# One layer of a hybrid encoder on one core: plain transposes in the input norm, a later hand-over of the state-space pieces, their output block in fixed order on another queue, and the first row tile's split in two parts

## The chip, the cores and the metric

One Trainium2 chip, one core. The metric is device time in microseconds of one execution; the kernel before took 1969.1 us, the median of three runs (1964.49 to 1969.29). The engines go by these names: PE or TensorE (matmul), DVE or VectorE, ACT or ScalarE, POOL or GpSimd, SP or SyncE (which issues most transfers). PSUM, where matmuls leave their results, has eight banks of 128 x 512 f32.

## The reference, cut to what matters

The input is 1024 rows of 1024 numbers. One layer is computed, in f32:

```
xn = rmsnorm(x) * g                       # over each row
p  = xn @ W_in                            # 1024 x 4896, cut into parts
y1 = S5(p[0:256]);  y2 = RG_LRU(p[256:768]);  y3 = GLA(p[768:1824])
merged = sum_b sigmoid(p_gate_b) * (y_b @ W_up_b)
h = x + merged @ W_mix_out
h = h + expert_choice_swiglu(rmsnorm(h))  # 16 experts, 128 rows each
out = rmsnorm(h)
```

S5, the state-space mixer, scans the sequence in both directions for 16 groups of 16 channels with 64 complex states each. Its output block is z = gelu(y), then z * sigmoid(z @ w_glu).

## The kernel before, in words

All of it is one function, written with a tile framework: the code issues instructions in a program order, and a planner puts them into each engine's queue when the program is built. It goes by priority (program order, unless a block says high priority) and by its own costs for when an instruction could start. Each engine then runs its queue strictly in that order, each instruction waiting for what it needs, and a transfer is issued from the queue of the engine that the code names. Inside a block marked `manual_schedule` each engine keeps the order of the code among the block's instructions; where instructions from outside the block come in between stays the planner's choice. Matmuls with f32 accuracy are made of three products of operands split into a high and a low part (`split`, line 52: ScalarE makes the high part, VectorE subtracts it).

**Prologue (lines 135 to 196, in manual order).** SyncE loads the rows x in four transfers of two 128-row tiles, then two 128-column blocks of W_in. For each row ScalarE sums squares (`sqs`, 143), VectorE adds epsilon and GpSimd raises to the power -0.5 (`chain`, 148; the power at line 81). Then VectorE makes a 128x128 tile `dg` for each row tile: the identity with the rows' factors on the diagonal (154). `xchunk(h, k)` (157) multiplies four 128x128 blocks of x with `dg` on TensorE (161), which transposes and scales at once, into one PSUM tile of 128x512 (`mx`, four buffers); ScalarE and VectorE split it into xnH and xnL (163). There are 16 chunks, eight for each half of the rows. Squares and chains for the second half stand between chunks of the first half, and the chain for the last four row tiles comes at once.

**Projections (line 380).** `proj` multiplies 128 columns of W_in with all rows: eight steps of k, three products, two halves, 48 matmuls into one of two PSUM tiles `pj`. `wsplit` (131) loads and splits the weights of the next one at high priority, and ScalarE evacuates the result (`evac`, 400, high priority), which SyncE stores to DRAM.

**State-space pieces (lines 486 to 654).** After the two projections for S5, a list of 13 tasks is driven: six projections for GLA, one larger one for its values (`col_va`), four for the LRU, two for the first gates. Behind each task `drive` (478) takes six pieces from the generator `s5_gen` (625). A batch of S5 has eleven: three that prepare coefficients on GpSimd and VectorE (`prep`, 505), then in `s5_batch` (530) transposes of W, small products that ScalarE copies out and SyncE stores as KD (567), loads of a Toeplitz tile TO from KD (571), state products, rotations, scans, rotations back, and the output products (609 and 615) with `Z` (620). Four batches, then the output block (631 to 652): gelu on Z in ScalarE, eight stores to ZD and one load back in another layout, both through SyncE, two f32 matmuls with w_glu for each half (643), tanh, a product, and the split into two `y` pairs. The first up-projection (`s5_out`, 676, matmuls at line 396) needs both.

**The end of the mixer (lines 973 to 1070).** Eight gates and up-projections of the LRU add to `merged` (128 x 8 x 1024, features in partitions). For the last feature block the addition is done first for the first 128 rows, then for the rest (1055 to 1058), and `msplit(t)` (1050) splits one 128-row tile of all eight feature blocks into MH and ML. The matmuls with W_mix_out start with tile 0 and feature block 0 (1087, matmuls at lines 68 to 70). The PSUM pools of the mixer are given back just before, and those of the next stage take their banks.

Behind it come router, selection of rows, and 16 experts with weights streamed from DRAM.

Of the kernel before, what the change touches and what calls it, by code (L numbers as in the profile page):

```python
# [8 lines left out]
F32 = mybir.dt.float32  # L9
# [3 lines left out]
AF = mybir.ActivationFunctionType  # L13
# [4 lines left out]
P = 128  # L18
S = 1024
D = 1024  # L20
KT = D // P
NT = S // P
# [15 lines left out]
def dram(t, off, ap):  # L38
    return bass.AP(tensor=t.tensor, offset=t.offset + off, ap=ap)
# [3 lines left out]
def hybrid_encoder(ctx: ExitStack, tc: tile.TileContext, A, out, dbg=None):  # L43
    nc = tc.nc
    v, g, s, te = nc.vector, nc.gpsimd, nc.scalar, nc.tensor
    dma = nc.sync.dma_start
    MUL, ADD, SUB = OP.mult, OP.add, OP.subtract

    def tap(name, ap):
# [3 lines left out]
    def act(o, i, f, bias=0.0, scale=1.0, **k):  # L53
        return s.activation(o, i, f, bias=bias, scale=scale, **k)  # L54

    def stt(o, a, c, b, op0, op1):
        return v.scalar_tensor_tensor(o, a, c, b, op0=op0, op1=op1)

    def split(h, lo, src, scale=None, eng=None):
        if scale is None:  # L60
            act(h, src, AF.Copy)
            (eng or v).tensor_tensor(lo, src, h.bitcast(F32), SUB)  # L62
        else:
            act(h, src, AF.Copy, scale=scale)
            stt(lo, src, scale, h.bitcast(F32), MUL, SUB)
# [13 lines left out]
    def rpow(o, x):  # L79

        g.tensor_tensor(o, x, mhalf.to_broadcast(list(x.shape)), OP.pow)
# [11 lines left out]
    def mx():  # L93
        return psum.tile([P, 512], F32, name="mx", bufs=4)
# [3 lines left out]
    idn = consts.tile([P, P], F32, name="idn")  # L98
# [7 lines left out]
    def ytile():  # L106
        return ypool.tile([P, S], F32R, name="y")
# [4 lines left out]
    xload = xlctx.enter_context(tc.tile_pool(name="xload", bufs=1, side="right", reuse_waits="tile"))  # L112
    x = A["x"][0]
    X = xload.tile([P, NT, D], F32, name="X")

    def xdma(t):
        dma(X[:, t:t + 2], x[t * P:(t + 2) * P].rearrange("(t p) d -> p t d", p=P))


    def wload(src, n):  # L120
        raw = xw.tile([P, KT, P], F32, name="wraw", bufs=2)
        dma(raw[:, :n], src.rearrange("(k p) c -> p k c", p=P))
        return raw, n

    def wconv(raw, n, eng=None):
        wh = xw.tile([P, KT, P], F32R, name="wh", bufs=2)
        wl = xw.tile([P, KT, P], F32R, name="wl", bufs=2)
        split(wh[:, :n], wl[:, :n], raw[:, :n], eng=eng)
        return wh, wl
# [8 lines left out]
    xnH = xw.tile([P, KT, S], F32R, name="xnH")  # L138
    xnL = xw.tile([P, KT, S], F32R, name="xnL")
    ss, rstd = (consts.tile([P, NT], F32, name=n) for n in ("ss", "rstd"))  # L140
    dg, first = [], []

    def sqs(t):
        for j in range(2):
            sq = xload.tile([P, D], F32, name="sq", bufs=2)
            act(sq, X[:, t + j], AF.Square, scale=1.0 / 32, accum_out=ss[:, t + j:t + j + 1])

    def chain(t, n):
        c = slice(t, t + n)
        v.tensor_scalar(ss[:, c], ss[:, c], EPS, None, op0=ADD)  # L150
        rpow(rstd[:, c], ss[:, c])
        for j in range(n):
            d_ = xload.tile([P, P], F32, name="dg", bufs=NT)
            v.tensor_scalar(d_, idn, rstd[:, t + j:t + j + 1], None, op0=MUL)
            dg.append(d_)

    def xchunk(h, k):
        hs = slice(h * 512, h * 512 + 512)
        ps = mx()
        for j in range(4):  # L160
            te.matmul(ps[:, j * P:(j + 1) * P], X[:, 4 * h + j, k * P:(k + 1) * P], dg[4 * h + j],
                      start=True, stop=True)
        split(xnH[:, k, hs], xnL[:, k, hs], ps, scale=gmix[:, k:k + 1])

    with tc.manual_schedule():
        dma(grow, A["mix_norm_g"].rearrange("l (k c) -> (l k) c", c=P))
        for t in range(0, NT, 2):
            xdma(t)
        raw0 = [wload(win[:, j * P:(j + 1) * P], KT) for j in range(2)]
        ps = mx()  # L170
        te.transpose(ps[:, 0:KT], grow, idn[:KT, :KT])
        v.tensor_copy(gmix, ps[:, 0:KT])
        for t in (0, 2):
            sqs(t)
            chain(t, 2)
        sqs(4)
        xchunk(0, 0)
        sqs(6)
        xchunk(0, 1)
        xchunk(0, 2)  # L180
        xchunk(0, 3)
        xchunk(0, 4)
        chain(4, 4)
        xchunk(0, 5)
        xchunk(0, 6)
        xchunk(0, 7)
        first.append(wconv(*raw0[0], eng=None))
        xchunk(1, 0)
        xchunk(1, 1)
        xchunk(1, 2)  # L190
        xchunk(1, 3)
        xchunk(1, 4)
        xchunk(1, 5)
        xchunk(1, 6)
        xchunk(1, 7)
        first.append(wconv(*raw0[1], eng=None))
    tap("xnH", xnH.bitcast(F32))
    tap("xnL", xnL.bitcast(F32))
# [31 lines left out]
    ps = mx()  # L230
# [7 lines left out]
    def tt(e, o, a, b, op=MUL):  # L238
        e.tensor_tensor(o, a, b, op)  # L239
# [35 lines left out]
    ps = mx()  # L275
# [55 lines left out]
    for n, src, sg in (("WR", PWR, 1), ("WI", PWI, 1), ("CR", PWR, 1), ("CI", PWI, 1), ("CN", PWI, -1)):  # L331
        t = sp.tile([P, 16, 8], F32, name="pq" + n)
# [29 lines left out]
    for n, sg in (("re", 1.0), ("im", -1.0)):  # L362
        ps = mx()
# [16 lines left out]
    def proj(c0):  # L380
        wh, wl = first.pop(0) if first else wsplit(win[:, c0:c0 + P], KT)
        ps = pj()
        for k in range(KT):
            for i, (w, xx) in enumerate(((wh, xnL), (wh, xnH), (wl, xnH))):
                for h in range(2):
                    te.matmul(ps[:, h], w[:, k], xx[:, k, h * 512:(h + 1) * 512],  # L386
                              start=(k == 0 and i == 0), stop=(k == KT - 1 and i == 2))
        return ps
# [11 lines left out]
    def evac(ps, dst, n=P):  # L400
        with tc.high_priority():
            ev = xw.tile([P, S], F32, name="ev", bufs=2)
            act(ev[:n], ps.rearrange("p a b -> p (a b)")[:n], AF.Copy)
            dma(dst, ev[:n])
# [3 lines left out]
    ZD = dpool.tile([256, 8, P], F32, name="ZD")  # L408
# [66 lines left out]
                "p (n s) -> p s n", s=8), AF.Copy)  # L475
            dma(UD[j * P:(j + 1) * P], ev.rearrange("p (s n) -> p s n", s=8))

    def drive(tasks, gen, n):
        for t in tasks:
            t()  # L480
            for _ in range(n):
                next(gen, None)
        for _ in gen:
            pass
# [3 lines left out]
    cols_rest = [lambda j=j: evac(proj(O_Q + j * P), GD[j * P:(j + 1) * P]) for j in (0, 1, 2, 3, 6, 7)]  # L488
# [6 lines left out]
    sw = s5ctx.enter_context(tc.tile_pool(name="s5w", bufs=1, side="right", reuse_waits="tile"))  # L495
# [3 lines left out]
    Z = sw.tile([P, 16, P], F32, name="Z")  # L499
# [125 lines left out]
    def s5_gen():  # L625
        for b in range(4):
            o = {}
            yield from prep(b, o)
            yield from s5_batch(b, o)
            yield  # L630
        act(Z, Z, AF.Gelu_apprx_tanh)
        for q in range(8):
            dma(dram(ZD, q * P, [[1024, 16], [16384, 16], [1, P]]), Z[q * 16:(q + 1) * 16])
        zT = sw.tile([P, 2, S], F32, name="Z")
        dma(zT, ZD.rearrange("(k p) t n -> p k (t n)", p=P))
        yield
        TT = sw.tile([P, 2, S], F32, name="U")
        for m in range(2):
            T = TT[:, m]
            for h in range(2):  # L640
                ps = mx()
                for k in range(2):
                    te.matmul(ps, wg[:, k, m * P:(m + 1) * P], zT[:, k, h * 512:(h + 1) * 512], start=not k, stop=bool(k))
                act(T[:, h * 512:(h + 1) * 512], ps, AF.Tanh, scale=0.5)
            stt(T, T, 1.0, zT[:, m], ADD, MUL)
            yh, yl = ytile(), ytile()
            nat = lambda z: z.rearrange("p (n t) -> p t n", t=8)
            per = lambda z: z.rearrange("p (t n) -> p t n", t=8)
            act(nat(yh), per(T), AF.Copy, scale=0.5)
            stt(nat(yl), per(T), 0.5, nat(yh.bitcast(F32)), MUL, SUB)  # L650
            ys5.append((yh, yl))
            yield

    drive(cols_rest, s5_gen(), 6)
    for i, (yh, yl) in enumerate(ys5):
        tap(f"ys5h{i}", yh.bitcast(F32))
        tap(f"ys5l{i}", yl.bitcast(F32))
# [7 lines left out]
    merged = mp.tile([P, KT, S], F32, name="merged")  # L665
# [372 lines left out]
    MH, ML = [], []  # L1038
# [8 lines left out]

    hload(H0, 0)
    load(0)
    def msplit(t):  # L1050
        split(MH[t], ML[t], merged[:, :, t * P:(t + 1) * P], scale=0.5)

    with tc.high_priority():
        G, U_ = (z.rearrange("p a b -> p (a b)") for z in (G, U_))
        for c in (slice(0, P), slice(P, S)):
            stt(G[:, c], G[:, c], 1.0, U_[:, c], ADD, MUL)
            tt(v, merged[:, KT - 1, c], merged[:, KT - 1, c], G[:, c], ADD)
            if c.start == 0:
                msplit(0)
        msplit(1)  # L1060
    tap("merged", merged)
    ps1ctx.close()
# [52 lines left out]
    for t in range(NT):  # L1115
        ps = bank("mo")
# [24 lines left out]
    for i in range(len(SH) - 3):  # L1141
        v.tensor_scalar(cst[:, i:i + 1], jf, float(2 ** SH[i + 1]), -float(sum(2 ** z for z in SH[:i + 1])),
                        op0=MUL, op1=ADD)
# [119 lines left out]
    with tc.manual_schedule():  # L1263
        v.tensor_scalar(ssq[:, 0], ssq[:, 0], 1.0 / D, EPS, op0=MUL, op1=ADD)
        lgen, sgen = iter(()), iter(())
        for t in range(NT):
            ps = bank("mo")
# [69 lines left out]
    with tc.manual_schedule():  # L1337
        for i, sh in enumerate(SH):
# [7 lines left out]
            ps = bank("mo")  # L1346
# [13 lines left out]
            if 2 * i >= len(late) and len(early_w) < XB:  # L1360
                n = len(early_w)
# [19 lines left out]
        for t in range(NT - 1):  # L1381
            te.matmul(pos[:, (t + 1) * 32:256], ones, G2[:, t:t + 1].to_broadcast([P, NT - 1 - t, 2, NE]), start=False,
                      stop=(t == NT - 2))
# [302 lines left out]
```

## Time and profile before

| What | Value |
|---|---|
| Median of three runs | 1969.1 us |
| Profiled execution, own time | 1967.92 us |
| Its span | 1966.1 us |
| TensorE busy | 1874.3 us, 95% |
| VectorE busy | 1499.7 us, 76% |
| ScalarE busy | 1166.8 us, 59% |
| GpSimd busy | 150.9 us, 8% |
| DMA | 495.94 MB, mean 252 GB/s |

The span begins with the first instruction that the profiler saw; the time has a little around it. A row of a timeline gives start, duration, engine (PEld is TensorE's weight load, SPq the queue of SyncE), source line, operation, the tiles written and read, and how many such instructions are merged in the row; in brackets stands how long the engine was idle just before and what ended that. The granted clock is 1.00 at 2.4 GHz and 0.50 at 1.2 GHz.

### The profile page before, as it was taken

How to read it: one execution, taken by the hardware profiler on the slowest of the kernel's cores; microseconds unless marked ns; L12 is line 12 of the kernel's file. 1: busy time of each engine (PE TensorE's matmuls, PEld its weight loads, DVE VectorE, ACT ScalarE, POOL GpSimd, SP SyncE). 2: the span in 40 equal slices, each digit the busy share in tenths (PEclk: the TensorE clock that was granted, in tenths of full speed). 3: DMA queues.
4: the chain of work that ended last, by engine and by line, in shares of the span. 5: the costliest groups of instructions: out<-in, count | busy, mean ns of one | idle time of the engine just before them, and what ended most of it. 6: DMA issues, size and time to landing. Idle time of an engine off the chain costs nothing.

```text
span 1966.1 us, 25361 instructions
## 1 busy us (share of the span) xinstructions
PE 1874.3 (95%) x9502; PEld 1539.3 (78%) x9502; DVE 1499.7 (76%) x1895; ACT 1166.8 (59%) x1380; POOL 150.9 (8%) x207
## 2 busy tenths in 40 slices
PE   7999989999899999579999999999999999999996
PEld 6878866777678878468888888888888888888884
DVE  6467225558875253789998999999899999999987
ACT  5221224435672132357787777877877777777785
POOL 1834000000000001000000000000000000000000
PEclk9999999999999999789999999999999999999998
DMA  6431331212212162869999999999999999999992
GB/s 173 104 101 38 98 95 29 80 31 70 67 39 88 32 220 108 325 259 374 391 381 383 391 381 379 381 388 384 386 389 380 379 383 391 384 385 386 385 357 96
DMA packets 263230, 495.94 MB, mean 252 GB/s; under 512 B 26756, under 2 KB 82468, under 8 KB 263108
## 3 DMA queue, kind: packets, MB, share of 16 engines
q1 hardware_dynamic: 255924, 468.64, 65.5%
q0 software_dynamic: 7184, 25.69, 4.4%
q8 instruction: 74, 1.21, 0.2%
q14 instruction: 48, 0.39, 0.1%
HBM read 464.55 MB, written 29.74 MB: 251 GB/s over the span
## 4 chain that ended last, share of the span: by engine, by line
PE 80%; DVE 6%; ACT 2%; issue 2%; DMA 1%; SPq 0%; POOL 0%; POOLq 0%; DVEq 0%; ACTq 0%
PE py L1482 17%; PE pj L386 12%; PE gu L68 12%; PE gu L70 12%; PE gu L69 11%; PE pj L396 3%; PE tp L1439 2%; PE mo L68 2%; PE mo L69 2%; PE mo L70 2%; ACT xwh L54 1%; DVE junk L1340 1%; DVE lr L949 1%; PE mx L808 0%; PE mx L801 0%
## 5 line engine op out<-in xcount | busy, mean ns | idle before, releaser
L239 DVE TENSOR_TENSOR xwl<-rawb,xwh 128x1024 fp32r<-128x1024 f32 x528 | 614.0, 1219 | 39.9 <-ACT xwh L54 39.0
L54 ACT ACTIVATE xwh<-rawb 128x1024 fp32r<-128x1024 f32 x528 | 521.8, 1052 | 14.1 <-PE gu L70 7.2
L68 PE MATMUL gu<-xwl,xeh 128*128 128x512 f32 x1024 | 406.9, 397 | 0.0
L70 PE MATMUL gu<-xwh,xel 128*128 128x512 f32 x1024 | 399.8, 390 | 0.0
L69 PE MATMUL gu<-xwh,xeh 128*128 128x512 f32 x1024 | 399.0, 390 | 0.0
L239 DVE TENSOR_TENSOR xwl<-rawa,xwh 128x1024 fp32r<-128x1024 f32 x192 | 226.2, 1220 | 25.3 <-ACT xwh L54 25.3
L70 PEld LDWEIGHTS gu<-xwh,xel 128*128 128x128 f32 x1024 | 192.4, 188 | 41.4 <-DVE xel L62 0.2
L69 PEld LDWEIGHTS gu<-xwh,xeh 128*128 128x128 f32 x1024 | 192.9, 188 | 37.7
L68 PEld LDWEIGHTS gu<-xwl,xeh 128*128 128x128 f32 x1024 | 192.7, 188 | 37.3 <-ACT xeh L54 0.2
L54 ACT ACTIVATE xwh<-rawa 128x1024 fp32r<-128x1024 f32 x192 | 192.9, 1052 | 7.1 <-PE py L1482 7.1
L386 PE MATMUL pj<-xnL,wh 128*128 128x512 f32 x576 | 181.7, 394 | 3.8 <-ACT ev L54 2.2
L386 PE MATMUL pj<-xnH,wl 128*128 128x512 f32 x576 | 181.0, 394 | 0.0
L386 PE MATMUL pj<-xnH,wh 128*128 128x512 f32 x576 | 180.4, 392 | 0.0
L54 ACT ACTIVATE wh<-wraw 128x1024 fp32r<-128x1024 f32 (+2 forms) x60 | 49.4, 827 | 193.3 <-PE pj L386 123.4
L1482 PE MATMUL py<-xwl,hTh 128*128 128x512 f32 x512 | 159.2, 392 | 3.6 <-DVE xwl L239 3.6
L1482 PE MATMUL py<-xwh,hTl 128*128 128x512 f32 x512 | 158.0, 390 | 0.5 <-DVE hTl L62 0.5
L1482 PE MATMUL py<-xwh,hTh 128*128 128x512 f32 x512 | 157.8, 389 | 0.0
L62 DVE TENSOR_TENSOR wl<-wraw,wh 128x1024 fp32r<-128x1024 f32 (+2 forms) x60 | 57.6, 962 | 107.4 <-ACT wh L54 96.1
L386 PEld LDWEIGHTS pj<-xnL,wh 128*128 128x128 f32 x576 | 107.4, 189 | 30.1 <-ACT ev L54 3.7
L386 PEld LDWEIGHTS pj<-xnH,wl 128*128 128x128 f32 x576 | 107.6, 188 | 25.5 <-issue 2.1
L386 PEld LDWEIGHTS pj<-xnH,wh 128*128 128x128 f32 x576 | 108.0, 188 | 24.4 <-issue 1.8
L1482 PEld LDWEIGHTS py<-xwl,hTh 128*128 128x128 f32 x512 | 94.9, 188 | 22.9 <-DVE xwl L239 2.5
(474 smaller groups left out, 2472.4 us busy)
## 6 DMA issues: line engine op xcount, KB each, us to landing
rawb<-in_w_exp_down_dram SPq DMA_DIRECT2D x90, 1024.0 KB, 8.3
rawb<-in_w_exp_up_dram SPq DMA_DIRECT2D x88, 1024.0 KB, 8.1
rawb<-in_w_exp_gate_dram SPq DMA_DIRECT2D x86, 1024.0 KB, 8.3
rawa<-in_w_exp_up_dram SPq DMA_DIRECT2D x40, 1024.0 KB
rawa<-in_w_exp_gate_dram SPq DMA_DIRECT2D x33, 1024.0 KB
rawa<-in_w_exp_down_dram SPq DMA_DIRECT2D x23, 1024.0 KB
wraw<-in_w_in_dram SPq DMA_DIRECT2D x36, 512.0 KB, 4.2
rawc<-in_w_exp_down_dram SPq DMA_DIRECT2D x15, 1024.0 KB
```

The costliest lines, as they stand in the source:

```text
L54: return s.activation(o, i, f, bias=bias, scale=scale, **k)
L62: (eng or v).tensor_tensor(lo, src, h.bitcast(F32), SUB)
L68: te.matmul(ps, lh, rl, start=first, stop=False)
L69: te.matmul(ps, lh, rh, start=False, stop=False)
L70: te.matmul(ps, ll, rh, start=False, stop=last)
L239: e.tensor_tensor(o, a, b, op)
L386: te.matmul(ps[:, h], w[:, k], xx[:, k, h * 512:(h + 1) * 512], start=(k == 0 and i == 0), stop=(k == KT - 1 and i == 2))
L396: te.matmul(ps[:, h], ww[:, k], yy[:, h * 512:(h + 1) * 512], start=(k == 0 and i == 0), stop=(k == len(ys) - 1 and i == 2))
L949: v.tensor_tensor_scan(rv(hh[d]), rv(hh[d]), rv(gi[d]), initial=0.0, op0=MUL, op1=ADD)
L1340: v.tensor_scalar(junk[:, half_], PT[:, half_], cand.bitcast(F32), 0.0, op0=OP.is_ge, op1=ADD, accum_out=cnt)
L1439: te.transpose(ps[:, j * P:(j + 1) * P], src[:, j * P:(j + 1) * P], idn)
L1482: te.matmul(E.py[:, h], a[:, j], b[:, h * 512:(h + 1) * 512], start=(f == 0 and j == 0 and p_ == 0), stop=(f == 3 and j == 3 and p_ == 2))
```

## The change

Four edits. In the prologue the rows are scaled in place by their factor on VectorE, and `xchunk` transposes them plainly with the identity; the chain for the last four row tiles is made in two pairs, and chunks are grouped between them (three, three, two). `drive` gets a parameter: behind the first two tasks no state-space piece is handed over, behind each later one seven in place of six. The gelu, the eight stores of ZD and the load stand in a block in manual order, and the nine transfers are issued from ScalarE's queue (`adma`). `msplit` takes a range of feature blocks; the first row tile is split for the first seven feature blocks ahead of the last additions, and for the eighth behind the first of them.

```diff
--- before.py
+++ after.py
@@ -43,7 +43,7 @@
 def hybrid_encoder(ctx: ExitStack, tc: tile.TileContext, A, out, dbg=None):
     nc = tc.nc
     v, g, s, te = nc.vector, nc.gpsimd, nc.scalar, nc.tensor
-    dma = nc.sync.dma_start
+    dma, adma = nc.sync.dma_start, nc.scalar.dma_start
     MUL, ADD, SUB = OP.mult, OP.add, OP.subtract
 
     def tap(name, ap):
@@ -138,7 +138,7 @@
     xnH = xw.tile([P, KT, S], F32R, name="xnH")
     xnL = xw.tile([P, KT, S], F32R, name="xnL")
     ss, rstd = (consts.tile([P, NT], F32, name=n) for n in ("ss", "rstd"))
-    dg, first = [], []
+    first = []
 
     def sqs(t):
         for j in range(2):
@@ -149,17 +149,14 @@
         c = slice(t, t + n)
         v.tensor_scalar(ss[:, c], ss[:, c], EPS, None, op0=ADD)
         rpow(rstd[:, c], ss[:, c])
-        for j in range(n):
-            d_ = xload.tile([P, P], F32, name="dg", bufs=NT)
-            v.tensor_scalar(d_, idn, rstd[:, t + j:t + j + 1], None, op0=MUL)
-            dg.append(d_)
+        for j in range(t, t + n):
+            v.tensor_scalar(X[:, j], X[:, j], rstd[:, j:j + 1], None, op0=MUL)
 
     def xchunk(h, k):
         hs = slice(h * 512, h * 512 + 512)
         ps = mx()
         for j in range(4):
-            te.matmul(ps[:, j * P:(j + 1) * P], X[:, 4 * h + j, k * P:(k + 1) * P], dg[4 * h + j],
-                      start=True, stop=True)
+            te.transpose(ps[:, j * P:(j + 1) * P], X[:, 4 * h + j, k * P:(k + 1) * P], idn)
         split(xnH[:, k, hs], xnL[:, k, hs], ps, scale=gmix[:, k:k + 1])
 
     with tc.manual_schedule():
@@ -174,25 +171,18 @@
             sqs(t)
             chain(t, 2)
         sqs(4)
-        xchunk(0, 0)
+        for k in range(3):
+            xchunk(0, k)
+        chain(4, 2)
         sqs(6)
-        xchunk(0, 1)
-        xchunk(0, 2)
-        xchunk(0, 3)
-        xchunk(0, 4)
-        chain(4, 4)
-        xchunk(0, 5)
-        xchunk(0, 6)
-        xchunk(0, 7)
+        for k in range(3, 6):
+            xchunk(0, k)
+        chain(6, 2)
+        for k in range(6, KT):
+            xchunk(0, k)
         first.append(wconv(*raw0[0], eng=None))
-        xchunk(1, 0)
-        xchunk(1, 1)
-        xchunk(1, 2)
-        xchunk(1, 3)
-        xchunk(1, 4)
-        xchunk(1, 5)
-        xchunk(1, 6)
-        xchunk(1, 7)
+        for k in range(KT):
+            xchunk(1, k)
         first.append(wconv(*raw0[1], eng=None))
     tap("xnH", xnH.bitcast(F32))
     tap("xnL", xnL.bitcast(F32))
@@ -475,10 +465,10 @@
                 "p (n s) -> p s n", s=8), AF.Copy)
             dma(UD[j * P:(j + 1) * P], ev.rearrange("p (s n) -> p s n", s=8))
 
-    def drive(tasks, gen, n):
-        for t in tasks:
+    def drive(tasks, gen, n, ahead=0):
+        for i, t in enumerate(tasks):
             t()
-            for _ in range(n):
+            for _ in range(n if i >= ahead else 0):
                 next(gen, None)
         for _ in gen:
             pass
@@ -628,11 +618,12 @@
             yield from prep(b, o)
             yield from s5_batch(b, o)
             yield
-        act(Z, Z, AF.Gelu_apprx_tanh)
-        for q in range(8):
-            dma(dram(ZD, q * P, [[1024, 16], [16384, 16], [1, P]]), Z[q * 16:(q + 1) * 16])
-        zT = sw.tile([P, 2, S], F32, name="Z")
-        dma(zT, ZD.rearrange("(k p) t n -> p k (t n)", p=P))
+        with tc.manual_schedule():
+            act(Z, Z, AF.Gelu_apprx_tanh)
+            for q in range(8):
+                adma(dram(ZD, q * P, [[1024, 16], [16384, 16], [1, P]]), Z[q * 16:(q + 1) * 16])
+            zT = sw.tile([P, 2, S], F32, name="Z")
+            adma(zT, ZD.rearrange("(k p) t n -> p k (t n)", p=P))
         yield
         TT = sw.tile([P, 2, S], F32, name="U")
         for m in range(2):
@@ -651,7 +642,7 @@
             ys5.append((yh, yl))
             yield
 
-    drive(cols_rest, s5_gen(), 6)
+    drive(cols_rest, s5_gen(), 7, 2)
     for i, (yh, yl) in enumerate(ys5):
         tap(f"ys5h{i}", yh.bitcast(F32))
         tap(f"ys5l{i}", yl.bitcast(F32))
@@ -1047,16 +1038,17 @@
 
     hload(H0, 0)
     load(0)
-    def msplit(t):
-        split(MH[t], ML[t], merged[:, :, t * P:(t + 1) * P], scale=0.5)
+    def msplit(t, k=slice(0, KT)):
+        split(MH[t][:, k], ML[t][:, k], merged[:, k, t * P:(t + 1) * P], scale=0.5)
 
     with tc.high_priority():
+        msplit(0, slice(0, KT - 1))
         G, U_ = (z.rearrange("p a b -> p (a b)") for z in (G, U_))
         for c in (slice(0, P), slice(P, S)):
             stt(G[:, c], G[:, c], 1.0, U_[:, c], ADD, MUL)
             tt(v, merged[:, KT - 1, c], merged[:, KT - 1, c], G[:, c], ADD)
             if c.start == 0:
-                msplit(0)
+                msplit(0, slice(KT - 1, KT))
         msplit(1)
     tap("merged", merged)
     ps1ctx.close()
```

## Rows read from the trace of the kernel before

**Rows 1.** Page, engines: busy us, share of the span, instructions.

```profile
PE 1874.3 (95%) x9502; PEld 1539.3 (78%) x9502; DVE 1499.7 (76%) x1895; ACT 1166.8 (59%) x1380; POOL 150.9 (8%) x207
```

**Rows 2.** Who waited, TensorE: line, waited for, us in total, times, longest us.

```profile
PE pj L396 <- DVE y L57: 5.1, 2, 2.7
...
PE mx L609 <- DMA TO<-KD: 4.4, 1, 4.4
...
PE mo L68 <- ACT MH L54: 2.7, 1, 2.7
```

**Rows 3.** Windows: us, PE, PEld, DVE, ACT, POOL busy (x); clock; DMA, GB/s.

```profile
126.10:129.50 3.40, 3.36 (x21) 2.94 (x22) 0.12 (x1) 0.00 (x0) 0.00 (x0) 0.50 0.02 5
...
261.00:264.00 3.00, 0.64 (x3) 0.22 (x2) 2.30 (x3) 2.31 (x4) 0.00 (x0) 1.00 0.00 0
...
269.50:272.60 3.10, 3.10 (x7) 2.46 (x8) 0.10 (x1) 1.01 (x1) 0.00 (x0) 0.50 0.00 0
...
690.75:693.48 2.73, 0.00 (x0) 0.00 (x0) 2.63 (x6) 1.11 (x2) 0.00 (x0) 0.86 0.50 128
...
693.48:699.40 5.92, 5.92 (x14) 4.40 (x15) 5.92 (x7) 5.92 (x7) 0.00 (x0) 0.50 1.05 400
```

**Rows 4.** Timeline, prologue: start us, duration us, engine, line, operation, count [idle before].

```profile
11.01 0.17 DVE L150 TENSOR_SCALAR ss<-ss 128x2 f32<-128x2 f32 x1 [1.13 <-ACT sq L54]
...
11.99 0.48 DVE L154 TENSOR_SCALAR dg<-idn,rstd 128x128 f32<-128x128 f32 x2 [0.81 <-POOL rstd L81]
...
22.33 2.07 DVE L57 SCALAR_TENSOR_TENSOR xnL<-mx,gmix,xnH 128x512 fp32r<-128x512 f32 x3
...
25.44 5.26 DVE L57 SCALAR_TENSOR_TENSOR xnL<-mx,gmix,xnH 128x512 fp32r<-128x512 f32 x7
...
26.25 3.84 PE L161 MATMUL mx<-dg,X 128*128 128x128 f32 x32
...
29.95 0.49 PE L386 MATMUL pj<-xnL,wh 128*128 128x512 f32 x1
...
32.38 0.66 PE L365 MATMUL mx<-idn,CNre 128*128 128x128 f32 x4
```

**Rows 5.** Groups by form: line, operation, shape, count, busy us, mean ns.

```profile
L898 DVE TENSOR_SCALAR xc<-xcl,cols 128x1024 f32<-128x1024 f32 x4 | 3.2, 811 | 3.0 <-DMA xcl<-LD 3.0
...
L940 DVE TENSOR_SCALAR lt<-lt 128x1024 f32<-128x1024 f32 x4 | 2.7, 684 | 0.0
```

**Rows 6.** Timeline, SyncE's queue, first state-space batch.

```profile
93.05 5.32 SPq L567 DMA_DIRECT2D KD<-kms  x8
...
120.94 1.48 SPq L571 DMA_DIRECT2D TO<-KD  x2
```

**Rows 7.** Timeline, ACT and SyncE's queue, state-space output block.

```profile
213.95 1.92 ACT L54 ACTIVATE Z<-Z 128x2048 f32<-128x2048 f32 x1 [3.66 <-DVE Z L57]
...
215.90 0.81 SPq L633 DMA_DIRECT2D ZD<-Z  x2
...
235.70 2.41 SPq L633 DMA_DIRECT2D ZD<-Z  x3
...
244.77 0.44 SPq L635 DMA_DIRECT2D Z<-ZD  x1
```

**Rows 8.** Timeline, PE and DVE, state-space output block.

```profile
253.69 7.03 PE L643 MATMUL mx<-Z,wg 128*128 128x512 f32 x16
...
267.42 2.00 DVE L57 SCALAR_TENSOR_TENSOR y<-U,y 128x1024 fp32r<-128x1024 f32 x1 [2.24 <-ACT y L54]
...
269.48 2.08 PE L396 MATMUL pj<-y,wh 128*128 128x512 f32 x4 [2.70 <-DVE y L57]
```

**Rows 9.** Chain that ended last, in order of time: start us, us, what.

```profile
641.78 10.88 PE pj L386 x48
...
690.85 1.28 DVE wmr L57 x2
...
692.37 1.06 ACT MH L54
```

## The prediction

> **What bounds the kernel now.** I read the page's engine line first: TensorE is busy 95% of a 1966.1 us span [rows 1], so time is won where TensorE stands still or runs at its lower clock, and nowhere else. Then the list of who waited, for TensorE alone [rows 2]: of its waits ahead of the expert stage, three belong to places that the change edits, for TO (state-space, first batch), for y (state-space output, two waits) and for MH (first row tile). Then the clock in short windows behind these [rows 3]: a granted clock of 0.50 is the 1.2 GHz level, and what is issued in such a stretch takes twice as long, so half of it is lost. Last the timelines and the chain at each place [rows 4, 6 to 9]. The three holes:
> - TO: 4.4 us of standing, then 3.40 us at 0.50, which loses 1.7. Together 6.1.
> - y: 5.1 us in two waits, 2.4 and 2.7 [rows 2]. Behind the first the clock is still 1.00 (261 to 264), behind the second 3.10 us run at 0.50 [rows 3], which loses 1.55. Together 6.6.
> - MH: 2.73 us of standing, then 5.92 us at 0.50, which loses 2.96 [rows 3]. Together 5.7.
>
> So TensorE's clock fell behind idle times of 2.7 us and more and stayed up behind one of 2.4.
>
> The sum goes against the profiled execution's own 1967.9 us (span 1966.1 and 1.8 around it); the median of the three runs is 1.2 higher.
>
> **The change part by part.**
>
> *Prologue.* Gone: eight diagonal tiles (0.48 us a pair [rows 4]) and their use as moving operand; new: eight in-place scalings of 128x1024 on VectorE. The same form in place takes 0.684 us, with two scalar columns 0.811 [rows 5]. TensorE's four products of a chunk took 3.84/4 = 0.96 us; four plain transposes take 0.66 at most [rows 4]. VectorE's own pace is 2.07/3 = 0.69 us a chunk where it is not kept waiting and 5.26/7 = 0.75 in the second half [rows 4]. Up to the second half's first chunk VectorE gets six scalings for six diagonal copies (6 x 0.684 - 3 x 0.48 = +2.7) and, since the last four rows are now done in two pairs, one more hand-over through GpSimd's power (11.01 to 11.99: +1.0), behind which the next chunk's subtraction stands in VectorE's queue; eight chunks go at 0.69 in place of 0.96 (-2.2). That is +1.5. Behind it, the last transposes need a PSUM buffer of four chunks earlier: 4 x (0.69 - 0.75) = -0.2 and 0.66 - 0.96 = -0.3. The first projection, which ran steadily from 29.95 [rows 4], then starts 0.9 us later. Ends: if VectorE is not the limit, 16 chunks go 0.27 faster, -4.3; with 0.811 a scaling, +1.7. I take +0.9, because both the scalings and the subtractions stand in one queue and the row of VectorE's pace is the nearer one.
>
> What the clock does there no row shows: at present the prologue's products are full matmuls. The Trainium skill ("TensorE: Matmul & The Clock Gate", Part 4: PE-mode transpose) says that transposes do not bring the clock to its upper level as matmuls do. By that rule the first projection would begin at 1.2 GHz; no stretch of this trace has transposes alone for long enough to tell. It is a rival below.
>
> *Hand-over.* The loop has 13 tasks and 47 pieces (11 for each of four batches, one for the output's activation and transfers, two for its gates). Piece i, counted from 0, was handed over behind task i//6 and is now handed over behind task 2 + i//7: the first batch's last piece moves from task 1 to task 3, the fourth batch's from 7 to 8, the output from 7 to 8. Nothing is added; what moves is, for each batch, GpSimd's products, the KD stores and eight TO loads on SyncE, and about a hundred short TensorE instructions. What it is worth is the TO hole. KD stores left SyncE only at 93.05 and the last TO loads at 120.94 [rows 6], because they stand behind weight loads that wait for buffers. Ends: -6.1 (two projections of 10.88 us [rows 9] go first and cover it), or +10.9 (the batches shift by a whole projection and the wait moves with them). I take 0: pieces handed over later meet the same weight loads in the same in-order queue, so the wait more likely moves than goes.
>
> *Output block.* Z's activation ends at 215.87; its eight stores left SyncE in groups of 2, 3 and 3 between 215.90 and 238.1, and the load at 244.77 [rows 7]. Between the groups SyncE held weight loads and evacuations that wait for a projection's end. Now the nine issues stand in order on ScalarE's queue. Their issue takes 0.41 to 0.80 us a store, so 3.2 to 6.4, and 0.44 for the load [rows 7]; behind them on ScalarE wait a weight split and an evacuation for each projection, for which VectorE and then TensorE wait, but a projection of 10.88 leaves room for both. If the stores follow the activation, the last leaves at 222.3, the load 6.7 later as now (238.1 to 244.8), at 229.0: 15.8 earlier. The output's matmuls, now at 253.69, could start at 237.9, or 248.8 if the hand-over costs them a projection. From their start to the first y were 10.1 us, to the second 15.7 (253.69 to 269.42 [rows 8]), so the y are there at 248 and 253.6, or 258.9 and 264.5; TensorE asks for them at about 261.4 and, six matmuls on, 262.8. Value: both waits and the low clock go, -6.6; in the later case 1.7 of it stays.
>
> *First row tile.* Behind the last projection product (690.75) TensorE waited for VectorE's gate sums (1.28, and 0.2 for the addition) and ScalarE's whole MH split (1.06) [rows 9]. Seven eighths of the split now need only sums that were done before; their work, about 1 us on either engine (the whole split is 1.06 on ScalarE), lies under the last 10.88 us of projection. TensorE's first matmul needs only the first eighth. What is late next is the PSUM bank of the last product, read by VectorE until 692.13. Ends: start at 690.8, -2.7 and -2.96; or no change, 0, if the early part finds no free place before 690.75. I take a start at 692.2, -1.3, and as 1.4 us of standing is less than the 2.4 behind which the clock stayed up, -2.96: -4.3.
>
> Sum: +0.9 + 0 - 6.6 - 4.3 = -10.0, so 1957.9 us for a profiled execution, 1959.1 on the scale of the median.
>
> **The rivals.**
> - *The TO wait goes as well*: -16.1, 1953.0. For it: two projections of independent matmuls now stand ahead of the first batch's last piece. Against: the planner, not the hand-over alone, chose the place, and it misjudged SyncE's queue.
> - *The stores stay scattered*: the order on ScalarE is fixed among these nine, but evacuations that wait for a projection's end may still stand between them, as on SyncE now. Then the y waits stay: -3.4, 1965.7. The Trainium skill ("DMA: Bandwidth & Descriptors", Issuing engines are not separate DMA queues) says that issuing from another engine saves only the sequencer's time; by that rule alone it would come out here too. The rows say that what delayed the stores was the wait between the groups, 28.9 us from first store to load, of which issuing is under 7.
> - *The prologue's clock*: the first projection starts at 1.2 GHz. The stretches of that level behind the three holes cost 1.55 to 2.96; I take 1.7 on top of the forecast, 1960.8.
> - *Slower*: the output comes a projection later and is as long as now. Its matmuls start at 264.6, the second y is there at 280.3, and TensorE, at 262.8, waits 17.5 and loses 1.55 of clock: 19.0 in place of 6.6, with the row tile and the prologue +9.0, 1978.1. It decides from a start of the output's matmuls later than 257.1 (3.4 later than now); the hand-over of the output behind task 8 in place of 7 speaks for it, the fixed order against it.
>
> **How the numbers follow.** Forecast 0.40, TO wait gone too 0.15, scattered stores 0.22, prologue's clock 0.11, slower 0.12. A measurement of this kernel tells 0.3% from no change, 5.9 us: faster is below 1963.2, slower above 1975.0. Faster are the forecast, the TO case and the clock case, 0.66; the planner orders everything behind anew, so I move some of it: faster 0.59, same 0.28, slower 0.13. The forecast's own range is 1954 (prologue at its lower end) to 1964 (only 1.3 at the row tile and some of the clock rival). The whole range: from 1950 (TO gone and part of the prologue's lower end) to 1970 (scattered stores, and 3 us of low clock and 0.8 of slower scalings in the prologue).
>
> **What would show it.** Right: the Z load leaves ScalarE less than 20 us behind the activation; TensorE has no wait for y over 1 us and 1.00 clock up to the next stage; the first row tile's matmul starts within 1.6 us of the last product at 1.00; the first projection starts between 29 and 32; a wait for TO of some 4 us remains. Wrong: weight splits or evacuations stand among the stores; TensorE stands longer for y than now; new waits of more than 5 us appear in the gated linear attention or recurrent stage, whose order the planner also sets anew; or the first ten us of projection run at 0.50.

## The result, and the profile after

The changed kernel takes 1978.43 us (median of six runs, 1977.42 to 1980.28), the kernel before 1969.19 beside it: ratio 1.0056, 95% interval 1.0044 to 1.0068. It is 11.0 us slower (8.7 to 13.4, the interval times 1969). Its profiled execution has a span of 1977.7 us, 11.6 over before. TensorE is busy as long as before (engines of the page; before: [rows 1]):

```profile
PE 1875.5 (95%) x9438; PEld 1535.2 (78%) x9438; DVE 1502.5 (76%) x1897; ACT 1167.0 (59%) x1381; POOL 151.1 (8%) x208
```

So the time went into standing still or into the lower clock. What TensorE waited for after (us in total, times, longest; before: [rows 2]). Line numbers are about ten lower from the prologue on; 634 is 643 of before, 386 is 396, 599 is 609:

```profile
PE mx L159 <- DVE X L153: 11.4, 5, 7.7
...
PE mx L634 <- DMA Z<-ZD: 5.3, 1, 5.3
...
PE pj L386 <- DVE y L57: 4.1, 2, 3.0
...
PE mx L599 <- DMA TO<-KD: 3.4, 1, 3.4
...
PE mo L70 <- DVE ML L57: 2.0, 1, 2.0
PE mx L599 <- DVE Z L57: 1.9, 1, 1.9
PE mx L605 <- DVE XSim L229: 1.7, 2, 1.2
```

The waits for y and TO are still there, and the wait for the output's load is new. Windows of 20 us of the kernel after (columns as in [rows 3]):

```profile
120.00:140.00 20.00, 16.64 (x127) 14.12 (x126) 5.70 (x11) 1.75 (x5) 3.45 (x7) 0.74 0.18 52
...
180.00:200.00 20.00, 16.10 (x81) 12.49 (x80) 15.72 (x28) 0.61 (x1) 5.76 (x8) 0.83 0.04 8
...
260.00:280.00 20.00, 13.18 (x31) 6.43 (x29) 2.31 (x3) 5.48 (x7) 0.00 (x0) 0.83 0.17 59
280.00:300.00 20.00, 17.39 (x67) 13.46 (x68) 9.72 (x14) 3.58 (x3) 0.53 (x1) 0.91 0.35 114
```

and the same windows of the kernel before:

```profile
120.00:140.00 20.00, 15.60 (x135) 13.17 (x134) 7.14 (x13) 2.59 (x7) 4.48 (x8) 0.91 0.22 59
...
180.00:200.00 20.00, 20.00 (x159) 16.84 (x158) 15.18 (x27) 3.61 (x7) 3.11 (x7) 1.00 0.09 23
...
260.00:280.00 20.00, 14.94 (x55) 11.01 (x54) 10.55 (x15) 6.89 (x7) 0.52 (x1) 0.91 0.23 59
280.00:300.00 20.00, 20.00 (x82) 14.88 (x81) 3.76 (x4) 10.60 (x12) 0.00 (x0) 1.00 0.30 99
```

A window's loss is what TensorE stood, plus its busy time by what the clock lacked. At 180 to 200: 3.9 + 16.1 x 0.17 = 6.6 where there was none. At 260 to 300: 9.4 + 3.8 = 13.2 in place of 6.4. At 120 to 140: 7.7 in place of 5.8. Together 15.3 more. The prologue, where TensorE's work itself changed, is left out of this sum; behind it ScalarE copies out the first projection 1.2 us earlier (at 42.41; before 43.59). Up to the end of the mixer the kernel after is 15.1 later (VectorE's first wmr, the gate sums of the last feature block, at 705.94; before 690.85 [rows 9]), so these windows explain all but about 1 us of it. From there to the end of the span it is 3.5 faster than before. ScalarE and its queue around the output block, kernel after (before: [rows 7]):

```profile
233.04 1.92 ACT L54 ACTIVATE Z<-Z 128x2048 f32<-128x2048 f32 x1
234.98 0.85 ACTq L624 DMA_DIRECT2D ZD<-Z  x2
...
241.59 0.81 ACTq L624 DMA_DIRECT2D ZD<-Z  x2
...
253.40 0.83 ACTq L624 DMA_DIRECT2D ZD<-Z  x1
...
263.67 0.39 ACTq L626 DMA_DIRECT2D Z<-ZD  x1
```

TensorE there (before: [rows 8]):

```profile
268.58 9.88 PE L634 MATMUL mx<-Z,wg 128*128 128x512 f32 x16 [5.28 <-DMA Z<-ZD]
281.49 2.05 PE L386 MATMUL pj<-y,wh 128*128 128x512 f32 x4 [3.03 <-DVE y L57]
```

The gelu starts 19.1 us later than before, and from first store to load it is 28.7 us as against 28.9: the batches arrive late, and the stores are as scattered as they were.

### The profile page after: what moved, and what is told of

Its sections match the earlier page's. It is cut to its first block, busy times and chain, and to the rows that moved or that the text cites. A ratio compares the mean times of both kernels' runs of the same rounds, so it can differ in the third digit from the quotient of the medians.

```text
span 1977.7 us, 25244 instructions
## 1 busy us (share of the span) xinstructions
PE 1875.5 (95%) x9438; PEld 1535.2 (78%) x9438; DVE 1502.5 (76%) x1897; ACT 1167.0 (59%) x1381; POOL 151.1 (8%) x208
## 4 chain that ended last, share of the span: by engine, by line
PE 86%; DVE 8%; ACT 3%; issue 2%; DMA 1%; SPq 0%; POOL 0%; POOLq 0%; DVEq 0%; ACTq 0%
PE py L1474 17%; PE pj L376 16%; PE gu L68 12%; PE gu L70 11%; PE gu L69 11%; PE pj L386 3%; PE tp L1431 2%; PE mo L68 2%; PE mo L70 2%; PE mo L69 2%; ACT xwh L54 1%; DVE junk L1332 1%; DVE lr L940 1%; PE mx L605 1%; PE mx L799 0%
```

## The experiments

Twelve kernels were run. A time in us is the ratio's distance from 1 times the median of before (1966 to 1968), with its 95% interval in brackets. Theory A1 was formed on the first four: what costs is where the planner puts the late batches' work in TensorE's queue. The count it rests on is that of projection matmuls (lines 386 before, 376 after) that stand ahead in TensorE's program order:

```
hand-over (pieces a task)      4th batch's   last output   output's   first state-space  measured
                               pieces behind products      matmuls    up-projection
                               tasks         behind        behind     behind
6 (before)                     5 to 7        491           669        672                0
7, none for two tasks          6 to 8        527           672        672                +13.2
6, none for two tasks          7 to 9        570           672        672                +17.7
11, none for two tasks         5             491           669        672                -1.8
```

**The four edits one by one**

*Prologue alone* (xchunk, chain and the order of the chunks as in the change).

> Before with the prologue part alone (rows scaled in place, plain transposes). Theory A, prologue gains a little: the first evacuation of a projection ended 1.2 us earlier in the changed kernel, so about 1968.0, -1.2 (between -0.5 and -2). Rival: what was gained by 42 us is given back, because the planner orders everything behind it anew and the first projections run 10 us at a granted clock of 0.66: 1969 to 1971.

Ratio 1.0005 (0.9994 to 1.0016): +0.9 us (-1.2 to +3.1). The prologue of that run, TensorE:

```profile
20.31 1.10 PE L159 MATMUL mx<-idn,X 128*128 128x128 f32 x6 [1.25 <-DVE xnL L57]
23.33 0.47 PE L159 MATMUL mx<-idn,X 128*128 128x128 f32 x1 [1.92 <-DVE X L153]
```

and its windows:

```profile
22.00:24.00 2.00, 0.67 (x2) 0.41 (x3) 1.48 (x3) 0.64 (x1) 0.48 (x1) 0.57 0.71 114
24.00:26.00 2.00, 2.00 (x11) 2.00 (x11) 2.00 (x3) 1.34 (x2) 0.00 (x0) 0.50 0.00 0
```

TensorE stands for the last pair's scalings, then transposes at 1.2 GHz until about 29. VectorE has work without a gap there (2.00 of 2.00 us busy), so the low clock can have cost little. The steady projection starts at 31.03, 1.1 later than before [rows 4], but six of its matmuls already stand between the transposes (one before), and ScalarE copies its result out earlier, not later: before, then this run:

```profile
43.59 1.03 ACT L54 ACTIVATE ev<-pj 128x1024 f32<-128x1024 f32 x1
```

```profile
42.75 1.03 ACT L54 ACTIVATE ev<-pj 128x1024 f32<-128x1024 f32 x1
```

That is 0.8 us (0.2 against the run with the row tile alone, which has the old prologue and copies out at 42.94). The first state-space batch gives it back, because GpSimd's coefficients are late:

```profile
65.85 0.66 PE L526 MATMUL mx<-idn,Wim 128*128 128x128 f32 x4 [1.57 <-POOL Wim L229]
```

So the gain up to 42 us is there, smaller than expected, and the rival's give-back behind it too, by this wait. The total is not clear of zero.

*Hand-over alone.*

```diff
-    drive(cols_rest, s5_gen(), 6)
+    drive(cols_rest, s5_gen(), 7, 2)
```

> Before with the hand-over alone (two tasks without pieces, then seven a task). Theory A, the hand-over is what costs: the output comes a projection later, its y waits stay or grow, and a hole of some 5 us opens behind the third batch: +10 to +16, 1979 to 1985, and the batches' output products stand 10 us or more later than before. Rival B, the stores on ScalarE's queue cost it: under +3, at most 1972. Rival C, the two only cost together: +3 to +8.

Ratio 1.0067 (1.0053 to 1.0081): +13.2 us (10.4 to 15.9). Its longest TensorE wait at the state-space block, and two windows:

```profile
PE mx L643 <- DMA Z<-ZD: 6.3, 1, 6.3
```

```profile
180.00:200.00 20.00, 16.75 (x123) 13.33 (x123) 13.85 (x20) 3.50 (x7) 5.77 (x8) 0.83 0.11 30
...
260.00:280.00 20.00, 11.69 (x28) 5.78 (x28) 4.36 (x3) 6.21 (x7) 0.00 (x0) 0.83 0.18 60
```

The two holes of the changed kernel are here, with the stores on SyncE. Theory A holds, rivals B and C fall.

*Output block alone* (manual order, transfers on ScalarE's queue).

> Before with the output block alone (manual order, nine transfers from ScalarE's queue). Theory A: the stores stay in groups between weight splits and evacuations, first store to load 25 us or more as before, and the y waits stay at about 5 us: 1967 to 1971. Rival B, the queue costs: weight splits stand behind stores and projections wait for them, over +6, 1975 or more. The prediction's own step would be -6.6, 1962.6.

Ratio 0.9991 (0.9981 to 1.0): -1.8 us (-3.7 to 0). Stores in groups of two, three, two and one between weight splits and evacuations, 217.90 to 245.25, the load at 248.17, two y waits of 4.8 in total: the mechanism of theory A, though the median of 1965.55 lies 1.5 below its range; rival B falls. The planner left the output's matmuls where they were, behind 668 projection matmuls (669 before).

*First row tile alone.*

> Before with the split of the first row tile alone. Theory A: the changed kernel's lead behind the mixer grew by 3.5 us at this place, and the clock stays at 1.00 behind it: 1965.7 (-3 to -4.5). Rival: the gain is given back in the expert stage, which streams its weights from memory: 1968 to 1969.5.

Ratio 0.9992 (0.9983 to 1.0001): -1.6 us (-3.3 to +0.2), less than expected and not clear of zero. The profiled executions resolve it better: from the first wmr to the end of the span it is 1274.6 to 1275.3 us without the split (before and the three runs above) and 1271.8 with it (here and in the changed kernel): -2.8 to -3.5.

The four add up to 0.9 + 13.2 - 1.8 - 1.6 = +10.7, against +11.0 for the whole change.

**What in the hand-over costs**

*Six a task, none for two tasks*: `drive(cols_rest, s5_gen(), 6, 2)`.

> Before with two tasks without pieces, then six a task as before. Theory A1, what counts is how many projection matmuls are left behind the last output products when they enter TensorE's queue: 491 stand ahead of them before, 527 with seven a task, 570 here, and the first state-space up-projection stands behind 672 in all three. The chain from the last output products to the first y took 51.6 us before (212.2 to 263.8); 102 matmuls of 0.227 us and 4 us of gates leave 25 us of it uncovered where 5 were: +13 to +22, 1981 to 1990, and the longest TensorE wait stands at the output block. Rival A2, seven a task crowd the batches and that opens the holes: under +5, 1973 at most.

Ratio 1.009 (1.0073 to 1.0107): +17.7 us (14.4 to 21.0). Its wait for the load:

```profile
PE mx L643 <- DMA Z<-ZD: 9.7, 1, 9.7
```

This is in theory A1's range, and A2 falls. Part of it is of another kind, though: TensorE also stands 5.4 us, until 198.75, in front of the third batch's first output product, until a transfer lands. The two shares were not separated.

*Eleven a task, none for two tasks*: `drive(cols_rest, s5_gen(), 11, 2)`.

> Before with two tasks without pieces, then eleven a task: one batch a task, so that the batches catch up. In TensorE's queue the last output products stand behind 491 projection matmuls again. Theory A1: no cost, 1966 to 1970 (-2 to +2), no hole at 180 to 200 us. Rival A3, to begin two projections later costs by itself: +8 to +13, 1976 or more. Rival A2, crowding: slower than the hand-over of seven a task, over 1981.

Ratio 0.9991 (0.9982 to 1.0): -1.8 us (-3.5 to 0). The first batch begins as late as in the change (its transposes of W stand behind 240 projection matmuls in place of 144; its output products stand behind 375 in all four), but the gelu starts where it did [rows 7], and 180 to 200 us is fully busy at 1.00:

```profile
213.93 1.92 ACT L54 ACTIVATE Z<-Z 128x2048 f32<-128x2048 f32 x1 [3.66 <-DVE Z L57]
```

So neither the later start (A3) nor more pieces a task (A2) costs anything, but the lag of the last batches does (A1). Seven a task without the pause gives the order of before on every engine; it was not run.

**What held up the output**

*Transfers from GpSimd's queue.*

```diff
-            dma(dram(ZD, q * P, [[1024, 16], [16384, 16], [1, P]]), Z[q * 16:(q + 1) * 16])
+            gdma(dram(ZD, q * P, [[1024, 16], [16384, 16], [1, P]]), Z[q * 16:(q + 1) * 16])
...
-        dma(zT, ZD.rearrange("(k p) t n -> p k (t n)", p=P))
+        gdma(zT, ZD.rearrange("(k p) t n -> p k (t n)", p=P))
```

> Before with the eight stores and the load issued from GpSimd's queue, which holds nothing else there, so they leave one behind the other: first store to load under 15 us in place of 28.9. Theory B1, the output's matmuls start where the planner put them in TensorE's queue and not when the load lands: they stand behind 652 projection matmuls in place of 669, so 3.9 us earlier, with no wait of their own; the first y wait goes, 1 to 2 us of the second stay, no low clock: -4 to -5.5, 1963. Rival B2, the load was what they waited for: they start 12 us or more earlier and both waits go, -6.6, 1961. Rival B3, the order behind it changes and gives it back: -1 to +1.

Ratio 0.9998 (0.9988 to 1.0007): -0.4 us (-2.4 to +1.4), less than expected. GpSimd's queue, then TensorE:

```profile
216.21 4.73 POOL L633 DMA_DIRECT2D ZD<-Z  x8 [28.76 <-ACT Z L54]
225.20 0.73 POOL L635 DMA_DIRECT2D Z<-ZD  x1 [4.25 <-DMA ZD<-Z]
```

```profile
249.88 7.03 PE L643 MATMUL mx<-Z,wg 128*128 128x512 f32 x16
...
265.49 1.38 PE L396 MATMUL pj<-y,wh 128*128 128x512 f32 x4 [2.68 <-DVE y L57]
```

The load leaves 9.0 us behind the first store and 19.6 us earlier than before, and the output's matmuls start 3.8 earlier, as their place behind 652 projection matmuls says, without a wait: B1 on the place, B2 falls. The first y wait is gone; the second and the low clock behind it stay. The time lies where B3 had it and is not clear of zero; whether something behind the output gives back the 2.4 us of the first wait is not shown.

*Stores over three queues.*

```diff
-            dma(dram(ZD, q * P, [[1024, 16], [16384, 16], [1, P]]), Z[q * 16:(q + 1) * 16])
+            (gdma, dma, gdma, nc.scalar.dma_start, gdma, dma, gdma, nc.scalar.dma_start)[q](dram(ZD, q * P, [[1024, 16], [16384, 16], [1, P]]), Z[q * 16:(q + 1) * 16])
...
-        dma(zT, ZD.rearrange("(k p) t n -> p k (t n)", p=P))
+        gdma(zT, ZD.rearrange("(k p) t n -> p k (t n)", p=P))
```

> Before with the eight stores shared out over the queues of GpSimd (four), SyncE (two) and ScalarE (two), the load on GpSimd's. Theory B1: the planner then puts the output's matmuls behind 596 projection matmuls in place of 669, 16.5 us earlier; if the load has landed by then, both y waits and the low clock go: -6.6, 1961 (1960 to 1963). Rival B3: the same waits go and the time stays within 1.5 of before, because something else is late there.

Ratio 0.9973 (0.9963 to 0.9983): -5.3 us (-7.3 to -3.3). TensorE waits for neither Z nor y:

```profile
239.00 7.03 PE L643 MATMUL mx<-Z,wg 128*128 128x512 f32 x16
263.10 1.07 PE L396 MATMUL pj<-y,wh 128*128 128x512 f32 x4
```

That is B1. The transfers are not what is faster here: from first store (217.74) to load (230.06) it is 12.3 us, more than the 9.0 on GpSimd's queue alone. The gain comes from the place that the planner now gives to the output's matmuls, behind 596 projection matmuls in place of 669.

**Together**

*The changed kernel with eleven a task*: `drive(cols_rest, s5_gen(), 11, 2)`.

> The changed kernel with one number altered: eleven pieces a task in place of seven, still none behind the first two tasks. Theory A1, the slowness is the lag of the third and fourth batch: their output products stand behind 414 and 491 projection matmuls again, the wait for the Z load and the hole at 180 to 200 us go, and the other three edits leave their single effects (+0.9, -1.7, -1.5): 1964 to 1968, some 11 to 13 under the changed kernel. Rival: the other edits add to it when they are together, or crowding: 1972 or more.

Ratio 0.9979 (0.9969 to 0.9988): -4.1 us (-6.1 to -2.4). One number turns the change from 11.0 slower to faster than before.

*The changed kernel with the stores over three queues.*

> The changed kernel with its hand-over of seven a task as it is, and the eight stores shared out over GpSimd's, SyncE's and ScalarE's queues, the load on GpSimd's. The output's matmuls then stand behind 634 projection matmuls in place of 672. If the lag costs through the output's y (5.3 us for the load, 4.1 for y and the low clock behind both), most of that goes and the hole at 180 to 200 us stays: 1966 to 1971. Rival: the lag costs before the output, in the batches: 1974 or more.

Ratio 0.9994 (0.9985 to 1.0004): -1.2 us (-3.0 to +0.8). The waits for Z and y are gone although the gelu is as late (228.90) as with the hand-over alone (228.76); what remains is at 180 to 200 us:

```profile
180.00:200.00 20.00, 16.08 (x114) 12.88 (x114) 12.80 (x18) 3.50 (x7) 5.76 (x8) 0.83 0.09 28
```

That is 6.7 by the sum above. Three queues gain 5.3 without the lag and 12.2 with it (from +11.0 to -1.2), so some 7 us of the lag's 13.2 are paid at the output and about as much in the hole before it, which this edit leaves as it was.

*The version that beats both*: before with the stores over three queues, eleven a task from the third task on, and the row tile's split.

> Before with three things: stores over three queues, eleven pieces a task from the third task on, the first row tile split in two. If the three are independent, -5.3, -1.8 and -1.5 to -3.5 add: 1957 to 1960 (-8 to -11). Rival, they share a hole: 1960 to 1962. TensorE then has no wait for y and none of 2.7 for MH; the wait for TO of 3 to 4 stays.

1958.24 us, ratio 0.9949 (0.9935 to 0.9963): -10.0 us (-12.8 to -7.3), as the sum of the three says. The y and MH waits are gone; a wait for TO of 2.3 and one for ML of 2.0 are left.

*The same with KD stores and TO loads dealt to two queues.*

```diff
-                dma(dram(KD, 4 * b * 240 + i * 16, [[3840, 16], [240, 4], [1, 16]]), src)
+                (dma, adma)[q % 2](dram(KD, 4 * b * 240 + i * 16, [[3840, 16], [240, 4], [1, 16]]), src)
...
-            dma(TO[q * 16:q * 16 + 16], dram(KD, 4 * b * 240 + (7 - q) * 16, [[3840, 16], [240, 4], [1, P]]))
+            (dma, adma)[q % 2](TO[q * 16:q * 16 + 16], dram(KD, 4 * b * 240 + (7 - q) * 16, [[3840, 16], [240, 4], [1, P]]))
```

> The version of the three things with the KD stores and TO loads of the four batches dealt in turn to SyncE's and ScalarE's queues, so that fewer weight loads stand between them. The planner then puts the first output products behind 328 projection matmuls in place of 375, the last behind 384 in place of 491. Theory, the TO hole is a matter of SyncE's queue: it goes, 4 to 6 us under the version without this, 1952 to 1955. Rival: in the earlier place the products wait for VectorE's rotations and scans instead; new holes of 5 us and more between 110 and 200 us, 1958 or more.

Ratio 1.0037 (1.0023 to 1.005): +7.3 us (4.5 to 9.8), some 17 above the version without this: the rival, but without a single hole of 5 us. The wait for TO is gone, as the theory said. TensorE's waits and windows:

```profile
PE mx L609 <- DVE Z L57: 4.7, 3, 2.1
...
PE mx L615 <- DVE XSim L239: 2.7, 3, 1.9
```

```profile
140.00:160.00 20.00, 18.19 (x119) 16.55 (x120) 10.05 (x16) 3.72 (x7) 11.38 (x13) 0.60 0.07 15
160.00:180.00 20.00, 17.33 (x118) 15.74 (x117) 15.90 (x27) 1.91 (x4) 6.04 (x9) 0.82 0.24 68
```

The planner took the batches forward by its own costs, and they came before VectorE's rotations were done: several short waits, the longest of 2.1, and a clock of 0.60 over 20 us.

## Why the prediction was wrong, step by step

**Hand-over: forecast 0, measured +13.2.** This is the step that failed. The prediction asked only about the TO hole, which indeed stayed (4.4 before, 3.4 after), and took it that pieces handed over later "meet the same weight loads in the same in-order queue". It had the fourth batch moving from task 7 to 8, but set no price on it, because the first batch's place seemed to decide. Eleven a task shows the opposite: the first batch may begin two projections later at no cost, as long as its output products keep their place. The other end matters, in two places. The first state-space up-projection stands behind 672 projection matmuls whatever is done, and from the last output products to its first y the kernel before needs 51.6 us (212.2 to 263.8). To cover them it had 181 projection matmuls of 0.227 us (41), the gates and small products, and still it stood 2.4 us before the first y. The change takes 36 of these matmuls away, 8.2 us, and its windows from 260 to 300 lose 6.8 more; six a task takes 79. The second place is the third batch. Its output products stand almost where they did (behind 414 to 422 projection matmuls; before 414), but VectorE comes to its last rotation 8.8 us later, before and after:

```profile
177.71 2.60 DVE L239 TENSOR_TENSOR XSim<-va,vb 128x256 f32<-128x256 f32 x2
```

```profile
186.55 2.57 DVE L229 TENSOR_TENSOR XSim<-va,vb 128x256 f32<-128x256 f32 x2
```

TensorE waits for it and for Z (1.7 and 1.9 us in the list above), and the window from 180 to 200 loses 6.6 with the low clock behind.

**Output block: forecast -6.6, measured -1.8.** Two steps failed. The stores did not follow the activation; manual order binds the nine to each other, but weight splits and evacuations still come between: the rival of scattered stores, to which the prediction gave 0.22. And the step from the load to the matmuls was wrong even where the stores do follow: the prediction let the matmuls start when the load is there, but in a queue that runs strictly in order they start at their place. The row of before could have told: L643 at 253.69 carries no wait in brackets [rows 8], 8.9 us after the load was issued [rows 7]. The term itself was rightly sized, as -5.3 with three queues shows. A smaller misreading: between the two waits for y TensorE has twelve matmuls, not six (263.78 to 266.78), so it asks for the second y some 1.6 us later than the prediction had it; this enters only the later cases. The Trainium skill ("DMA: Bandwidth & Descriptors", Issuing engines are not separate DMA queues) counts another issuing engine as a gain in sequencer time alone. Here the eight issues were 3.2 to 6.4 us of 28.9, and GpSimd's queue brought 28.9 down to 9.0, because nothing stood between them; what that was worth came from the place that the planner then gave to the matmuls.

**First row tile: forecast -4.3, measured -1.6 (-3.3 to +0.2), by the profiles -2.8 to -3.5.** Right in mechanism, with the standing mis-sized. The clock stays at 1.00. But VectorE's seven eighths of ML did not go under the last projection; the queue has them behind the gate sums wmr. VectorE after, then TensorE:

```profile
705.94 1.28 DVE L57 SCALAR_TENSOR_TENSOR wmr<-wmr,pj 128x128 f32<-128x128 f32 x2 [13.37 <-PE pj L386]
707.14 1.08 DVE L57 SCALAR_TENSOR_TENSOR ML<-merged,MH 128x896 fp32r<-128x896 f32 x1
```

```profile
705.90 0.40 PE L69 MATMUL mo<-wmh,MH 128*128 128x512 f32 x1
708.28 0.50 PE L70 MATMUL mo<-wmh,ML 128*128 128x512 f32 x1 [1.98 <-DVE ML L57]
```

VectorE idles 13.37 us in front of the gate sums with that work queued behind them. Two matmuls go at once and the third waits 2.0 us, where the prediction had 1.4. The PSUM bank, which it had named as late next, was not. That the clock would stay up was taken from the length of the standing alone, and this does not carry: behind 1.98 us here it stayed at 1.00, around the 1.92 us in the prologue it fell to 0.50.

**Prologue: forecast +0.9, measured +0.9 (-1.2 to +3.1).** The agreement is luck. The start of the steady projection did come 0.8 (after) and 1.1 (alone) later, as summed, but six of its matmuls had gone ahead of it, and its result was there 0.8 (alone) and 1.2 (after) us earlier. What was lost again, 1.6 us in front of the first batch's Wim, is not in the prediction, and with the hand-over of the change this wait does not arise. The clock rival was half right: TensorE ran transposes at 0.50 behind the 1.9 us wait, until about 29 us, but the steady projection starts at 1.00. The Trainium skill ("TensorE: Matmul & The Clock Gate", Part 4: PE-mode transpose) says that transposes do not bring the clock to its upper level. The trace agrees in that 17 transposes from 24.03 on did not bring it up; from 12 to 20 us, however, the clock was 1.00 with transposes alone.

**The sum.** The rival on the slower side gave 1978.1 with its mechanism named (a projection later, the output's matmuls at 264.6 and the second y at 280.3; they came at 268.6 and 286.8), at a chance of 0.12. That its sum meets the measured 1978.4 is luck in the parts: it put 12.4 more at the output, where the windows show 6.8 more, and the 6.6 at 180 to 200 us it did not have. It spoke of the output's hand-over alone; what moved it was the fourth batch ahead of it, and a second hole that was on no list.

## What to carry to other kernels

When a planner interleaves two streams, ask where the last piece of the moved stream lands in the in-order queue and how many instructions are left between it and its first consumer; the first piece says little. An instruction without a wait in front of it starts at its place in the queue, so bringing its data earlier is worth only what the planner makes of it. The fastest chain of transfers (GpSimd's empty queue) gained nothing clear of noise, and a slower one over three queues gained 5.3, because it moved the consumer's place: look at the place before the chain.

## What the runs showed of the hardware

The same wait had different lengths of low clock behind it. Behind the wait for TO (4.40 us before, 4.12 in the run with the row tile alone, the same queue order up to there), kernel before:

```profile
126.00:128.00 2.00, 1.86 (x10) 1.66 (x12) 0.00 (x0) 0.00 (x0) 0.00 (x0) 0.53 0.04 8
128.00:130.00 2.00, 2.00 (x19) 1.68 (x15) 0.61 (x2) 0.00 (x0) 0.00 (x0) 0.62 0.00 0
130.00:132.00 2.00, 2.00 (x20) 1.63 (x19) 0.00 (x0) 0.00 (x0) 0.00 (x0) 1.00 0.00 0
```

and with the row tile alone:

```profile
130.00:132.00 2.00, 2.00 (x12) 1.55 (x13) 0.00 (x0) 0.00 (x0) 0.00 (x0) 0.50 0.00 0
132.00:134.00 2.00, 2.00 (x14) 1.78 (x13) 1.23 (x4) 0.40 (x1) 0.27 (x4) 0.50 0.00 0
134.00:136.00 2.00, 2.00 (x16) 1.90 (x15) 1.88 (x3) 0.80 (x2) 0.00 (x0) 0.83 0.00 0
```

Some 3.4 us at 0.50 in the one [rows 3] and 9 in the other. The gelu stands 1.6 us earlier in before (213.95 and 215.57), the first wmr 2.5 (690.85 and 693.31). The profile that the prediction summed against was thus one of the better executions, and single profiles of these kernels differ by some 2 us with no difference in their order. What decides between the two stayed open.
